# One encoder layer on one core: w_xq's transposes over four PSUM banks, w_xo's middle pieces in the weight ring, sums of x's third chunk behind a cast, and the patterns' sums turned a step later

## The chip, the cores and the metric

The kernel runs on one core of one Trainium2 chip. Time is device time in microseconds (us). The core has TensorE (PE; its weight loads are PEld), VectorE (DVE), ScalarE (ACT), GpSimd (POOL) and SyncE (SP), which work off their own queues in order, and sixteen DMA engines. SP issues most transfers and POOL the rest; a transfer that waits holds up all that is queued behind it on its issuer.

## The reference

One layer of a bidirectional encoder over 2048 tokens of width 1024, in float32:

```python
y = rmsnorm(x, g_mix) @ w_in                     # q, k, v (8 heads of 64) and the conv's a, g
att = sum over 3 dilated window patterns of weights * attention(q, k, v)
conv = silu(layernorm(depthwise_conv31(a * sigmoid(g))))
h = x + concat(att, conv) @ w_out
xq = rmsnorm(h, g_x) @ w_xq                      # 4 heads of 256
xk, xv = rmsnorm(mem, g_mem) @ w_xk, ... @ w_xv  # 256 memory tokens
h = h + softmax(xq xk^T / 16) xv @ w_xo
h = h + square(relu(rmsnorm(h, g_mlp) @ w_up)) @ w_down
out = rmsnorm(h, g_final)
```

The weights of the patterns are a softmax over the logarithms of the three patterns' denominators.

## The kernel before

Matrix products are made in three passes from a high and a low part of each operand (hi x hi, lo x hi, hi x lo: `mm3`, L270 to L272). A high part is a cast on ScalarE (`xh`, `whi`, `lwhi`), a low part a subtraction on VectorE or GpSimd (`xl`, `wlo`, `lwlo`).

The tokens go in four chunks of 512 (numbered 0 to 3; what the change's title calls the third chunk is `xprep(sp, 2)`). For a chunk, `xprep` loads x, sums its squares on ScalarE (L381, tile `junk`), makes the inverse root `rsx` on VectorE, spreads it over partitions by TensorE transposes (`rb`, copied to `rbs`), transposes x (`xt`), stores the transposed x (`xts` to `xscr`, by SP), and multiplies and splits it into `xh` and `xl`. The input linear then makes 128 columns of w_in for a chunk at a time: `glu` units (a and g columns; `sig` is the sigmoid of g's columns and `u` the product), then q and k (kr and qr are the columns that rope turns), then v. `linear` takes a PSUM bank of the kind "mm"; the bank is free again when its reader (`sig`, `u`, a rope operation) is done.

`qkscale` reads the q and k columns of w_in once more, in 16 loads by SP (tiles `qks`), squares them on ScalarE (L781) and sums the partitions on TensorE (`qkp`, L789); the scale of the q and k weights comes from that. `mem` prepares the memory tokens.

The order in each queue is written by hand. The work is given as Python generators; `weave(main, (side, rate))` takes a step of main and then rate steps of each side, `pinned(gen, names)` puts a generator's instructions behind the ones that `last` holds under these names, and `after` does it for one block. A simulated timeline then sets the order of what is not pinned, so that a pin moves neighbours as well. `steps` is the stream of linear units, `later` the chunks 2 and 3 of x and the memory, `qks` the scale's generator.

In the attention stage the far patterns run with a filler beside them: the class `Matrices` makes, for cross attention, products of the weights with the memory. Its 32 pieces are 0 to 15 (w_xk and w_xv, `proj`), 16 to 23 (w_xq) and 24 to 31 (w_xo). `turn` transposes a head's two pieces of w_xq on TensorE, four 128x128 blocks to a bank (`xqt`, L539), ScalarE casts the high half (`whi_m`, L541) and VectorE makes the low half (`wlo_m`, L542), which frees the bank. `score` makes the product with the memory's keys (`pa`). `back` multiplies w_xo's pieces with the memory's values (`pb`) and stores the result (`eb` to `bscr`, by POOL). PSUM's banks in this stage are mm 0 and 1, S 3 and 4 (scores), T 5 and 6 (`pt`, the transposed probabilities, and `catT`) and O 7 and 2.

`load` brings a piece into the ring "raw" of the pool `wp`, which has two slots, or for some pieces into tiles of their own in the pool `bl`, which is opened when the filler has ended. `split` casts the piece and makes its low half (`whi_m` L261, `wlo_m` L262). After `backs` come the first two pieces of w_out (`ahead`, `raw_o`, `whi_o`) in the same ring "raw".

`combine` sums the three patterns of a head pair `pr` and a chunk `p`: it loads two of them (`ld`), works out the weights (`ce`, `csm`) and the sum (`cat`) on GpSimd, transposes it on TensorE (`catT`, L1178) and splits it (`ct`) for the product with w_out. Chunk 0 is done in the stage above; for 1 to 3 it runs beside the later stages.

Of the kernel before, what the change touches and what calls it, by code (L numbers as in the profile page):

```python
# [24 lines left out]
H = 8  # L25
# [22 lines left out]
def hybrid_layer(ctx, tc, A, out):  # L48
# [27 lines left out]
    last = {}  # L76
# [31 lines left out]
    def drain(*gens):  # L108
        for g in gens:
            for _ in g:  # L110
                pass
# [345 lines left out]
    class Matrices:  # L457
# [8 lines left out]
        def load(self, i):  # L466
            if i >= 32 or i in self.ring:
                return
            if 25 < i < 30:
                raw = self.bl.tile([P, 2, 512], F32, tag=f"rb{i}", name=f"raw_m{i}")  # L470
            else:
                raw = wp.tile([P, 8, P] if i < 24 else [P, 2, 512], F32, tag="raw", name=f"raw_m{i}", bufs=2)
            if i < 24:
                src = wcols((w_xk, w_xv, w_xq)[i // KC], i % KC * P)
            else:
                h, nh = divmod(i - 24, 2)
                src = w_xo[256 * h:256 * h + 256, 512 * nh:512 * nh + 512].rearrange("(e p) m -> p e m", p=P)
            dma(raw, src, nc.gpsimd)
            self.ring[i] = raw
# [50 lines left out]
        def turn(self, h):  # L530
            self.wt = []
            for e in range(2):
                i = 16 + 2 * h + e
                raw = self.ring.pop(i)
                whi, wlo = (wp.tile([P, 8, P], F32R, tag=f"w{q}", name=f"w{q}_m{i}", bufs=2) for q in ("hi", "lo"))
                for g in range(2):
                    pt = ps("mm", f"xqt{i}{g}")
                    for x in range(4):
                        PE.transpose(pt[:, x * P:(x + 1) * P], raw[:, 4 * g + x, :], ident)  # L539
                    hv = whi[:, 4 * g:4 * g + 4, :].rearrange("p a b -> p (a b)")  # L540
                    ACT.copy(hv, pt)  # L541
                    DVE.tensor_tensor(wlo[:, 4 * g:4 * g + 4, :].rearrange("p a b -> p (a b)"), pt, f(hv),  # L542
                                      op=ALU.subtract)
                    yield
                self.load(i + 2)
                self.wt.append((whi, wlo))
# [18 lines left out]

        def back(self, i):
            h, nh = divmod(i - 24, 2)
            if i < 26:
                self.load(i + 6)
            wh, wl = self.ring.pop(i)  # L570
            vt = self.vt
            for mc in range(2):
                ms = slice(mc * P, (mc + 1) * P)
                pt = ps("mm", f"pb{h}{nh}{mc}")
                for e in range(2):
                    mm3(pt, vt[h][:, 0, e, ms], vt[h][:, 1, e, ms], wh[:, e], wl[:, e], e == 0, e == 1)
                if mc == 0:
                    self.split(i + 1)
                ev = zp.tile([P, 512], F32, tag=f"z{(2 * i + mc) % 8}", name=f"eb{h}{mc}{nh}")
                if mc:  # L580
                    DVE.tensor_scalar(ev, pt, rmem[:, 1:2], None, op0=ALU.mult)
                else:
                    ACT.activation(ev, pt, AF.Copy, scale=rmem[:, 0:1])
                dma(bscr[4 * nh:4 * nh + 4, :, 2 * h + mc, :].rearrange("m p c -> p m c"),
                    ev.rearrange("p (m c) -> p m c", c=P), nc.gpsimd)
                yield
# [348 lines left out]
    with ExitStack() as st:  # L935
        sp = pool("stage", stack=st)
        cwt = conv_weights()
        next(cwt)
        setup()
        four = glu_first(sp, (0, 1))  # L940
        x0, x1 = xprep(sp, 0), xprep(sp, 1)
        next(four)
        next(x0)
        next(four)
        next(x1)
        next(four)
        next(four)
        next(four)
        next(four)
        next(cwt)  # L950
        x0, x1 = pinned(x0, "pgain", "gain"), pinned(x1, "pgain", "gain")
        next(x0)
        behind("sumsq", pinned(four, "rsx0"))
        behind("split", four)
        with ExitStack() as st0:
            after(st0, "rbt0", "rsx0")
            next(four)
        next(x0)
        pins = {1: (), 3: ("x0_3",), 5: ("xt0_5", "xv0_4"), 6: ("x0_5",)}
        for k in range(KC - 1):  # L960
            behind(f"x0_{k}", x1)
            next(x0)
            if k in pins:
                with ExitStack() as st0:
                    after(st0, *pins[k])
                    next(four)
        drain(x0)
        with ExitStack() as st0:
            after(st0, "x0_6", "xt0_7")
            drain(cwt)  # L970
        next(x1)
        behind("x0_6", four)
        with ExitStack() as st0:
            after(st0, "xt0_7", "xv0_6")
            next(four)
        next(x1)
        next(four)
        last["flo"] = last["lo"]
        early01 = (0, 1)
        units = [four] + [u for c in range(2, 4) for u in glu(c, early01)]  # L980
        units += [lin_qk(isq, c) for c in ("r", 0, 1, 2) for isq in (False, True)]
        ready = {}

        def hook():
            ready["gated"] = pipeline(*(u for c in range(4) for u in glu(c, (2, 3), True)))
            next(ready["gated"])
            ready["mats"] = Matrices()

        steps = pipeline(*units, lin_v(hook), stage={0: 4})
        with ExitStack() as st0:  # L990
            after(st0, "rb1", "xl0_3")
            next(steps)
        drain(islice(steps, 10))
        weave(islice(steps, 20), (x1, 0.5))
        drain(x1)
        mem = memory(sp)
        later = pinned(chain(xprep(sp, 2), islice(mem, 1), xprep(sp, 3), mem), "x1_7", "flo", "pe")
        qks = pinned(qkscale(), "x1_7", "xs1")
        weave(islice(steps, 34), (later, 0.4), (qks, 0.2))
        weave(islice(steps, 7), (later, 2.4), (qks, 0.7))  # L1000
        drain(later, qks)
    with ExitStack() as st0:
# [118 lines left out]
    def combine(p, pr, o0):  # L1121
# [48 lines left out]
                W.tensor_tensor(at, at, src, op=ALU.add)  # L1170
        yield
        yield
        ct = [cats[0][x, pr] if end else aq.tile([P, 512], F32R, tag=f"ct{x}", name=f"ct{x}{p}{pr}") for x in "hl"]
        with ExitStack() as st:
            after(st, "pe", "act", "dve")
            pt = ps("T", f"catT{p}{pr}")
# [175 lines left out]
    with ExitStack() as st:  # L1352
        p2_ = pool("att_far", stack=st, side="right")
        qlow3 = low_parts(p2_, S, 2, "ql3")
        gated, mats = ready["gated"], ready["mats"]
# [3 lines left out]
        def filler():  # L1359
# [6 lines left out]
            for h in range(XH):  # L1366
                yield from mats.turn(h)
                yield from islice(gated, 8)
                yield from mats.score(h)
            mats.split(24)  # L1370
            yield from gated

        def backs():
# [31 lines left out]
        xp_ = pool("post_x", stack=dense)  # L1405
        with ExitStack() as st1:
            mats.bl = pool("back_w", stack=st1)
            for i in range(26, 30):
                mats.load(i)
            load_cat(0, 0)  # L1410
            load_cat(0, 1)
            weave(pinned(backs(), "pe"), (first, 0.55))
# [639 lines left out]
```

## Time and profile before

| | |
|---|---|
| three runs, median | 2781.64 us (2779.82 to 2792.18) |
| the profiled execution | 2778.42 us, its span 2776.6 us |
| mean granted TensorE clock | 0.993 |
| HBM traffic over the span | 384.46 MB read, 148.52 MB written |

The profile is of one execution. Rows of the timeline have start and length in us, engine, line, operation, tile written and tiles read, and in brackets the idle time before it with what ended it; a row with x3 stands for three in a stretch, and the length is then that of all. The tables of windows give length, busy time of each engine (with the number of instructions), granted clock, share of the sixteen DMA engines and GB/s. The input linear's stage is the first 390 us, attention with its filler 390 to 655 us, `backs` about 655 to 690 us, and w_out starts after that.

### The profile page before, as it was taken

The page shows a single profiled execution, that of the slowest core. Times are in us where ns is not written, and L with a number is a line of the kernel's source. Part 1 is how long each engine was busy: PE and PEld are TensorE (multiplying, and loading weights), DVE is VectorE, ACT ScalarE, POOL GpSimd, SP SyncE. Part 2 cuts the span into 40 slices and gives each one's busy share as a digit, 9 for nine tenths or more (in the row PEclk, how much of TensorE's full clock was granted, in tenths as well). Part 3 has the DMA queues.
Part 4 walks back from the last instruction along what each step waited for, and adds up shares of the span by engine and source line. Part 5 has one row for each costly group of instructions (what it writes and reads, how often), then busy time and mean ns, then how long its engine had stood idle before and what let it go on. Part 6 is the DMA issues. An engine that isn't in the chain of part 4 may idle for free.

```text
span 2776.6 us, 40568 instructions
## 1 busy us (share of the span) xinstructions
PE 2686.4 (97%) x14783; PEld 2073.0 (75%) x14783; DVE 1905.0 (69%) x3485; ACT 1261.7 (45%) x2162; POOL 588.0 (21%) x807
## 2 busy tenths in 40 slices
PE   7999999998999999999999999999999999999998
PEld 4444457776778888787888788887887788878787
DVE  4678726665798776588985588665566776666765
ACT  6742227655454333434544434454344444444435
POOL 6564323543002212201111101121010122200000
PEclk9999999999999999999999999999999999999999
DMA  7875457887536666766467777764434554484553
GB/s 255 229 189 117 132 183 194 255 244 235 179 115 208 214 221 202 241 212 202 133 206 228 247 224 232 238 217 152 138 114 144 186 193 163 166 300 152 164 181 106
DMA packets 459816, 535.67 MB, mean 193 GB/s; under 512 B 98173, under 2 KB 329201, under 8 KB 459617
## 3 DMA queue, kind: packets, MB, share of 16 engines
q1 hardware_dynamic: 420992, 406.52, 48.6%
q0 software_dynamic: 36752, 123.06, 12.6%
q10 hardware_dynamic: 1872, 3.52, 0.3%
q8 instruction: 116, 1.90, 0.3%
q14 instruction: 84, 0.68, 0.1%
HBM read 384.46 MB, written 148.52 MB: 192 GB/s over the span
## 4 chain that ended last, share of the span: by engine, by line
PE 69%; DMA 9%; issue 8%; DVE 7%; ACT 3%; POOL 3%; SPq 2%; ACTq 0%; POOLq 0%; DVEq 0%
PE b L1750 7%; PE dn L270 4%; PE dn L271 4%; PE dn L272 4%; PE up L270 3%; PE up L272 3%; PE up L271 3%; PE lin L270 2%; PE lin L272 2%; PE lin L271 2%; PE pt L1038 2%; SPq L57 2%; PE s L1231 2%; PE x L271 1%; PE x L270 1%
## 5 line engine op out<-in xcount | busy, mean ns | idle before, releaser
L287 DVE SCALAR_TENSOR_TENSOR cacc<-cu,cwu,cacc 128x512 f32<-128x512 f32 x480 | 396.7, 828 | 6.5
L1032 ACT ACTIVATE sm<-sm,o 128x256 f32<-128x256 f32 (+1 forms) x384 | 160.0, 467 | 112.2 <-DVE o L1031 111.9
L270 PE MATMUL up<-mh,whi_u 128*128 128x512 f32 x512 | 203.9, 398 | 0.0
L270 PE MATMUL dn<-hhh,whi_d 128*128 128x512 f32 x512 | 201.6, 404 | 1.1 <-ACT hhh L1586 1.1
L271 PE MATMUL dn<-hhl,whi_d 128*128 128x512 f32 x512 | 199.9, 393 | 0.8 <-DVE hhl L1587 0.8
L272 PE MATMUL up<-mh,wlo_u 128*128 128x512 f32 x512 | 200.0, 391 | 0.0
L271 PE MATMUL up<-ml,whi_u 128*128 128x512 f32 x512 | 199.7, 390 | 0.0
L272 PE MATMUL dn<-hhh,wlo_d 128*128 128x512 f32 x512 | 198.9, 391 | 0.0
L1031 DVE CUSTOM_DVE_ANT_0 sm<-s,mask 128x256 f32<-128x256 f32 (+1 forms) x384 | 127.0, 375 | 29.7 <-PE s L1231 11.1
L1042 DVE TENSOR_TENSOR pl<-pt,ph 128x512 f16<-128x512 f32 x160 | 109.8, 687 | 48.4 <-ACT ph L1041 48.0
L247 POOL TENSOR_TENSOR nr<-st_v,mhalf 128x4 f32<-128x4 f32 x12 | 13.5, 1126 | 596.4 <-DVE st_v L243 596.4
L1601 DVE TENSOR_TENSOR h<-h,dn 128x512 f32<-128x512 f32 x128 | 86.4, 684 | 69.8 <-PE dn L272 69.2
L1041 ACT CAST ph<-pt 128x512 f16<-128x512 f32 x160 | 92.6, 579 | 78.9 <-PE pt L1038 78.1
L272 PEld LDWEIGHTS up<-mh,wlo_u 128*128 128x128 f32 x512 | 96.1, 188 | 20.4
L272 PEld LDWEIGHTS dn<-hhh,wlo_d 128*128 128x128 f32 x512 | 96.2, 188 | 20.1
L271 PEld LDWEIGHTS dn<-hhl,whi_d 128*128 128x128 f32 x512 | 96.4, 188 | 19.5 <-DVE hhl L1587 1.7
L271 PEld LDWEIGHTS up<-ml,whi_u 128*128 128x128 f32 x512 | 96.3, 188 | 18.6
L270 PEld LDWEIGHTS up<-mh,whi_u 128*128 128x128 f32 x512 | 96.2, 188 | 18.6
L270 PEld LDWEIGHTS dn<-hhh,whi_d 128*128 128x128 f32 x512 | 95.3, 188 | 19.7 <-ACT hhh L1586 2.2
L270 PE MATMUL o<-cath,whi_o 128*128 128x512 f32 x256 | 102.6, 402 | 3.3 <-ACT whi_o L261 2.5
L271 PE MATMUL o<-catl,whi_o 128*128 128x512 f32 x256 | 101.0, 395 | 1.7 <-DVE catl L1181 1.7
L270 PE MATMUL x<-pth,whi_b 128*128 128x512 f32 x256 | 100.4, 398 | 2.4 <-ACT xp L1510 1.4
(632 smaller groups left out, 7975.2 us busy)
## 6 DMA issues: line engine op xcount, KB each, us to landing
raw_u<-in_w_up_dram SPq DMA_DIRECT2D x64, 512.0 KB
raw_d<-in_w_down_dram SPq DMA_DIRECT2D x64, 512.0 KB
k<-kscr SPq DMA_DIRECT2D x32, 640.0 KB
raw_a<-ascr SPq DMA_DIRECT2D x32, 512.0 KB
raw_b<-bscr SPq DMA_DIRECT2D x32, 512.0 KB
lou<-wlo_u POOLq DMA_DIRECT2D x32, 512.0 KB, 5.5
lod<-wlo_d POOLq DMA_DIRECT2D x32, 512.0 KB, 5.7
wlo_u<-lou SPq DMA_DIRECT2D x32, 512.0 KB
```

The source lines that it names most:

```text
L57: return (q or nc.sync).dma_start(o, i)
L270: PE.matmul(o, lh, rh, start=first, stop=False)
L271: PE.matmul(o, lh, rl, start=False, stop=False)
L272: last["pe"] = PE.matmul(o, ll, rh, start=False, stop=end)
L287: DVE.scalar_tensor_tensor(acc, u[:, t:t + 512], cwu[:, c, t:t + 1], acc, op0=ALU.mult, op1=ALU.add)
L1031: last["dve"] = DVE.tensor_tensor_reduce(dst, so, mask[:, 256 * m:256 * m + nk], 1.0, 3e38, ALU.add, ALU.min, mn)
L1032: last["act"] = ACT.activation(dst, dst, AF.Exp, bias=mn, scale=-1.0)
L1038: last["pe"] = PE.transpose(pt[:, j, :], sm[:, j, :], ident)
L1041: ACT.copy(ph, pt)
L1042: DVE.tensor_tensor(pl, pt, ph, op=ALU.subtract)
L1601: last["dve"] = DVE.tensor_tensor(hs[m], hs[m], pt, op=ALU.add)
L1750: PE.matmul(o, w[i][:, k, :], Y[b][q][k], start=first and k + x == 0, stop=k == 3 and x == 2, skip_group_check=not first)
```

## The change

Four edits, apart from each other:

```diff
@@ load
-            if 25 < i < 30:
+            if i > 27:
                 raw = self.bl.tile([P, 2, 512], F32, tag=f"rb{i}", name=f"raw_m{i}")
@@ turn
-                    pt = ps("mm", f"xqt{i}{g}")
+                    pt = ps("T" if g else "mm", f"xqt{i}{g}")
@@ back
-            if i < 26:
-                self.load(i + 6)
             wh, wl = self.ring.pop(i)
...
                     self.split(i + 1)
+                    if i == 24:
+                        self.load(27)
@@ the input linear's order
         drain(islice(steps, 10))
+        last["g2"] = last["split"]
         weave(islice(steps, 20), (x1, 0.5))
...
-        later = pinned(chain(xprep(sp, 2), islice(mem, 1), xprep(sp, 3), mem), "x1_7", "flo", "pe")
+        later = pinned(chain(xprep(sp, 2), islice(mem, 1), xprep(sp, 3), mem), "x1_7", "g2", "flo", "pe")
...
-        weave(islice(steps, 34), (later, 0.4), (qks, 0.2))
+        weave(islice(steps, 8), (later, 0.4))
+        weave(islice(steps, 26), (later, 0.4), (qks, 0.32))
@@ combine
         yield
         yield
+        if p and pr < H // 2 - 1:
+            yield
@@ filler
             mats.split(24)
+            mats.load(26)
@@ before backs
-            for i in range(26, 30):
+            for i in range(28, 32):
                 mats.load(i)
```

**The third edit on ScalarE.** In the early stage, behind the casts of x's second chunk, ScalarE has these rows before (numbers behind names are the program's; `ssx2` and `ssx3` are the sums of the chunks 2 and 3, g20 a piece of w_in's g columns):

```order
L381 ACTIVATE junk_934,ssx2_933<-xn2_0_0_911 128x512
L381 ACTIVATE junk_936,ssx2_933<-xn2_0_1_912 128x512
L381 ACTIVATE junk_938,ssx2_933<-xn2_1_0_915 128x512
...
L781 ACTIVATE qks00_960,qka_959<-qks00_960 128x512
L381 ACTIVATE junk_942,ssx2_933<-xn2_2_0_919 128x512
L781 ACTIVATE qks01_963,qka_959<-qks01_963 128x512
L381 ACTIVATE junk_944,ssx2_933<-xn2_2_1_920 128x512
L381 ACTIVATE junk_946,ssx2_933<-xn2_3_0_923 128x512
L381 ACTIVATE junk_948,ssx2_933<-xn2_3_1_924 128x512
L381 ACTIVATE junk_1276,ssx3_1275<-xn3_0_0_1211 128x512
L226 CAST lwhi_g20_693<-lraw_g20_679 128x1024
L672 ACTIVATE sig0_1_988<-lin_899,wscl_328 128x512
```

and after the change these:

```order
L226 CAST lwhi_g20_693<-lraw_g20_679 128x1024
L381 ACTIVATE junk_934,ssx2_933<-xn2_0_0_911 128x512
L672 ACTIVATE sig0_1_981<-lin_899,wscl_328 128x512
L381 ACTIVATE junk_936,ssx2_933<-xn2_0_1_912 128x512
L781 ACTIVATE qks00_1003,qka_1002<-qks00_1003 128x512
L225 ACTIVATE lraw_a20_691<-lraw_a20_691,wscl_328 128x1024
L781 ACTIVATE qks01_1006,qka_1002<-qks01_1006 128x512
L381 ACTIVATE junk_938,ssx2_933<-xn2_1_0_915 128x512
L781 ACTIVATE qks10_1030,qka_1002<-qks10_1030 128x512
L781 ACTIVATE qks11_1033,qka_1002<-qks11_1033 128x512
L226 CAST lwhi_a20_1253<-lraw_a20_691 128x1024
L781 ACTIVATE qks20_1072,qka_1002<-qks20_1072 128x512
```

The cast `lwhi_g20` and `sig0_1` come to the head, the squares of chunk 2 are spread out behind them, and qks reads and the scaling and cast of a20 come among them; the squares of chunk 3 come later. On TensorE `qkp` moves ahead by 140 rows, to the front of the g3 linear, and `rb2` back by some 250. On SP the stores of chunk 2's first two transposes (`xts2`) come ahead of the first qks load. The transposes of x's chunk 3 move back into the linears kr1 to kr3, and the last `rope_qr` of VectorE's rows near 186 us comes eleven rows earlier.

**The second edit on POOL.** Before, from the last store of `ascr` to the first piece of w_out (the sums of the patterns and two stores of u between them left out):

```order
L57 DMA ascr_110<-ea33_7195 128x2x256
L57 DMA raw_m30_7798<-in_w_xo_dram 128x2x512
L57 DMA raw_m31_7834<-in_w_xo_dram 128x2x512
...
L57 DMA bscr_111<-eb000_7811 128x4x128
L57 DMA bscr_111<-eb010_7821 128x4x128
L57 DMA raw_m26_7772<-in_w_xo_dram 128x2x512
L57 DMA raw_m27_7774<-in_w_xo_dram 128x2x512
L57 DMA raw_m28_7776<-in_w_xo_dram 128x2x512
L57 DMA raw_m29_7778<-in_w_xo_dram 128x2x512
L57 DMA bscr_111<-eb001_7847 128x4x128
...
L57 DMA bscr_111<-eb201_7998 128x4x128
L57 DMA raw_o00_8093<-in_w_out_dram 128x8x128
```

After:

```order
L57 DMA ascr_110<-ea33_7195 128x2x256
L57 DMA raw_m26_7205<-in_w_xo_dram 128x2x512
L57 DMA raw_m27_7811<-in_w_xo_dram 128x2x512
...
L57 DMA bscr_111<-eb000_7813 128x4x128
L57 DMA bscr_111<-eb010_7823 128x4x128
L57 DMA raw_m28_7774<-in_w_xo_dram 128x2x512
L57 DMA raw_m29_7776<-in_w_xo_dram 128x2x512
L57 DMA raw_m30_7778<-in_w_xo_dram 128x2x512
L57 DMA raw_m31_7780<-in_w_xo_dram 128x2x512
L57 DMA raw_o00_8093<-in_w_out_dram 128x8x128
L57 DMA bscr_111<-eb001_7847 128x4x128
L57 DMA bscr_111<-eb011_7857 128x4x128
L57 DMA raw_o01_8099<-in_w_out_dram 128x8x128
```

The two early loads are pieces 26 and 27 in place of 30 and 31, the four at the start of `backs` are 28 to 31, and the first piece of w_out comes nine rows earlier, directly behind them.

**The first edit on TensorE.** The transposes of pieces 16 and 17 in the attention stage before (matmuls only, whole groups shortened to their first row):

```order
L539 MATMUL xqt160_5825<-ident_307,raw_m16_5654 128x128 x4
L1231 MATMUL s_5832<-k3_3_4990,qh3_3_4992 128x256
...
L1038 MATMUL pt_5849<-ident_307,sm_5763 128x128 x4
L1046 MATMUL opt_5787<-v2_01_4978,ph_5783 128x65
...
L539 MATMUL xqt161_5842<-ident_307,raw_m16_5654 128x128 x4
...
L539 MATMUL xqt170_5876<-ident_307,raw_m17_5747 128x128 x4
L539 MATMUL xqt171_5883<-ident_307,raw_m17_5747 128x128 x4
L270 MATMUL lin_5919<-xh0_2_903,lwhi_g22_5206 128x512
```

and after:

```order
L539 MATMUL xqt160_5825<-ident_307,raw_m16_5654 128x128 x4
L1235 MATMUL s_5832<-k3_3_4990,qh3_3_4992 128x256
...
L539 MATMUL xqt161_5842<-ident_307,raw_m16_5654 128x128 x4
L1048 MATMUL opt_5787<-v2_01_4978,ph_5783 128x65
...
L1040 MATMUL pt_5849<-ident_307,sm_5763 128x128 x4
L1050 MATMUL opt_5787<-v2_01_4978,pl_5784 128x65
...
L539 MATMUL xqt170_5876<-ident_307,raw_m17_5747 128x128 x4
L1101 MATMUL s3_5893<-k3_4_5519,qh3_4_5521 128x128
...
L539 MATMUL xqt171_5883<-ident_307,raw_m17_5747 128x128 x4
```

`xqt161` moves ahead of `pt` and of its `opt` group, `xqt170` ahead of the scores `s3`, and `xqt171` behind six matmuls of the linear.

The fourth edit moves `catT` and its split a few units later for chunks 1 to 3 and the first three head pairs.

## The prediction

> **What bounds the kernel now.** I read the page first, then the chain's view, TensorE's waits, a table of windows, and the timelines of the stretches where the waits are.
>
> ```profile
> span 2776.6 us, 40568 instructions
> PE 2686.4 (97%) x14783; PEld 2073.0 (75%) x14783; DVE 1905.0 (69%) x3485; ACT 1261.7 (45%) x2162; POOL 588.0 (21%) x807
> PE 69%; DMA 9%; issue 8%; DVE 7%; ACT 3%; POOL 3%; SPq 2%; ACTq 0%; POOLq 0%; DVEq 0%
> ```
>
> TensorE is busy for 97% of the span and carries 69% of the chain that ended last. The change neither adds nor removes a matmul, so it can only win or lose time in which TensorE stands still or runs at half clock. The view of TensorE's waits (total, times, longest) gives the prices that the four edits can touch:
>
> ```profile
> PE xqt L539 <- DVE wlo_m L542: 6.1, 5, 1.8
> PE catT L1178 <- POOL cat L1170: 4.9, 3, 2.2
> PE pb L270 <- ACT whi_m L261: 4.1, 1, 4.1
> PE lin L270 <- ACT sig L672: 3.8, 1, 3.8
> PE rb L255 <- DVE rsx L250: 2.6, 2, 1.5
> PE o L270 <- ACT whi_o L261: 2.5, 1, 2.5
> PE lin L270 <- DVE rope_qr L874: 2.3, 1, 2.3
> PE pb L271 <- DVE wlo_m L262: 0.8, 1, 0.8
> ```
>
> Some waits cost more than their length, because the granted clock falls behind them. Four short windows (length; PE, PEld, DVE, ACT, POOL busy; clock; DMA share; GB/s) follow the sig wait, the rope_qr wait, the whi_m wait and the whi_o wait:
>
> ```profile
> 76.50:79.90 3.40, 3.21 (x10) 1.73 (x11) 2.15 (x8) 3.40 (x9) 1.06 (x2) 0.50 0.82 239
> 189.10:192.50 3.40, 3.20 (x8) 1.14 (x8) 3.33 (x4) 2.49 (x5) 3.40 (x3) 0.50 0.82 191
> 663.60:670.40 6.80, 6.07 (x16) 4.47 (x17) 2.75 (x4) 2.53 (x3) 0.75 (x1) 0.50 0.98 345
> 690.90:694.30 3.40, 3.40 (x9) 2.62 (x9) 3.04 (x5) 1.04 (x1) 0.86 (x1) 0.50 1.05 329
> ```
>
> At a clock of 0.50 half the window is lost: 1.7, 1.7, 3.4 and 1.7 us. A wait of 2.3 us lost the clock here as one of 4.1 did. The Trainium skill ("TensorE: Matmul & The Clock Gate", Part 1) says that the clock halves after at least one idle window of about 3.4 us; by that rule the 2.3 us and 2.5 us waits would have kept it, and the new wait that I find below would cost no clock. The trace speaks against it, so I keep 1.7 us as a possible surcharge on any wait over 2.3 us.
>
> **The early stage (third edit).** First TensorE, then ScalarE, then SP's queue with ScalarE's waits for qks in all (us, times), in before:
>
> ```profile
> 70.52 0.38 PE L271 MATMUL lin<-xl,fhi_a 128*128 128x512 f16 x1
> 70.73 0.38 PE L272 MATMUL lin<-xh,flo_a 128*128 128x512 f16 x1
> 70.95 0.28 PE L213 MATMUL sqs_a<-sqv_a,small 128*128 128x1 f32 x2
> 75.03 0.38 PE L270 MATMUL lin<-xh,lwhi_g 128*128 128x512 f16 x1 [3.81 <-ACT sig L672]
> 76.69 1.11 PE L255 MATMUL rb<-ident,rsx 128*128 128x128 f32 x4 [1.06 <-DVE rsx L250]
> ```
>
> ```profile
> 62.47 0.62 ACT L381 ACTIVATE junk<-xn 128x512 bf16<-128x512 f32 x1
> 68.58 0.63 ACT L781 ACTIVATE qks<-qks 128x512 f32<-128x512 f32 x1 [3.13 <-DMA qks<-in_w_in_dram]
> 73.37 1.03 ACT L226 CAST lwhi_g<-lraw_g 128x1024 f16<-128x1024 f32 x1
> 74.30 0.68 ACT L672 ACTIVATE sig<-lin,wscl 128x512 f32<-128x512 f32 x1
> 76.79 1.15 ACT L225 ACTIVATE lraw_a<-lraw_a,wscl 128x1024 f32<-128x1024 f32 x1
> 85.17 1.05 ACT L208 ACTIVATE sqj_a<-lraw_a 128x1024 bf16<-128x1024 f32 x1
> 104.06 0.19 ACT L781 ACTIVATION_READ_ACCUMULATOR qks<-qks 128x1 f32 x1
> ```
>
> ```profile
> 61.65 1.07 SPq L57 DMA_DIRECT2D qks<-in_w_in_dram  x2
>   DMA qks<-in_w_in_dram: 7.1, 3
> ```
>
> From 62.47 ScalarE works off x's squares (junk), waits 3.13 us for the first qks piece, and only then makes lwhi_g and sig. TensorE stands still for 3.81 us, then 1.06 us for x2's rsx, and loses 1.7 us of clock: 6.6 us. After the change lwhi_g and sig stand at the head of that stretch and rb comes some 250 TensorE rows later, so these 6.6 us go. What is late next?
>
> (a) The second bank. The next linear's second bank is freed by u (DVE), which now stands behind the column chain from sqs_a at 70.95. TensorE would want the bank at about 71.6; I allow 1 us, an estimate, 0 to 2.
>
> (b) qkp. It moves ahead by 140 rows, from behind the g3 linear's first half to its very front. A linear's matmul starts every 0.215 us (70.52, 70.73), and between sqs_a and qkp now stand 96 of them, 20.7 us: TensorE arrives at 71 + 1 + 20.7 = 92.7 us. The last of the product with the sig's bank lies 7 matmuls before sqs_a, so sig can run at about 69.5 us. From there until lwhi_g's next cast, ScalarE has 4 sigs at 0.6 (2.4), 6 squares at 0.8 with their accumulator reads (4.8), 16 qks at 0.65 (10.4), two scalings at 1.1 (2.2), one square of a column at 1.05, and two casts at 0.95 (1.9): 22.8 us, so 92.3 us with nothing to wait for, and 1.2 us for the cast's low half: 93.5. But the qks loads start later: on SP they now stand behind the stores of x2's first two transposes, which stand 23 matmuls and a set of transposes before sqs_a, at 65.5 us; with copy and issue, 66.5 instead of 61.65. In before the first load was read 6.9 us after its issue (61.65 to 68.58), so the first read comes at 73.4 instead of about 71, and the end goes to about 95.3. TensorE waits 2.6 us. Ends: 0, if loads come in time; 6.5, if qks waits again for DMA in between. The clock surcharge of 1.7 may come with it.
>
> (c) x's third chunk. Its transposes, sums and casts move into the kr linears, and the kr3 linear reads it. Sixteen VectorE operations, each of a size with the rope_qr row's 0.68 us (below), so 11 us, stand between the first rope and the last of them, and two linears of 24 matmuls, 10.4 us, is the time they have. I take 2 us, 0 to 5.
>
> Sum of the early stage: -6.6 + 1 + 2.6 + 2 = -1.0 us, from -6.6 to +8.6.
>
> A second effect is on the 186 us wait. VectorE stood in two taps when rope_qr came up:
>
> ```profile
> 184.35 4.29 DVE L287 SCALAR_TENSOR_TENSOR cacc<-cu,cwu,cacc 128x512 f32<-128x512 f32 x2
> 188.57 0.68 DVE L874 TENSOR_TENSOR rope_qr<-lin,rope_qr 128x512 f32<-128x512 f32 x1
> ```
>
> The last rope_qr now stands 11 rows earlier on VectorE, ahead of five taps and the v scale's column work. The 2.3 us and their 1.7 us of clock can go; I take 3 us, 0 to 4.
>
> **w_xq's transposes (first edit).** Each matrix has two groups of four transposes; the next group's bank comes free when VectorE has made the low half (wlo_m) of the one two groups back. TensorE, then VectorE:
>
> ```profile
> 553.50 0.63 PE L539 MATMUL xqt<-ident,raw_m 128*128 128x128 f32 x4 [0.38 <-PE s L1231]
> 555.43 0.63 PE L539 MATMUL xqt<-ident,raw_m 128*128 128x128 f32 x4 [1.30 <-DVE wlo_m L542]
> 554.61 1.28 DVE L542 TENSOR_TENSOR wlo_m<-xqt,whi_m 128x512 fp32r<-128x512 f32 x2
> ```
>
> With four banks the last group no longer needs the first's. 6.1 us are in the row of waits; four heads hold most of it. What it pays: pt uses the same T pair, so a pt now follows the previous pt's low half (pl). In the new order pt stands after the two matmuls that need only the high half, and the next one needs pl anyway, so the wait would come there without it. I take 5 us, 2 to 6.1.
>
> **w_xo's pieces (second edit).** POOL's issues, and the cast that waited:
>
> ```profile
> 656.71 2.83 POOL L57 DMA_DIRECT2D raw_m<-in_w_xo_dram  x4
> 680.01 0.91 POOL L57 DMA_DIRECT2D raw_o<-in_w_out_dram  x1
> 661.97 1.04 ACT L261 CAST whi_m<-raw_m 128x1024 fp32r<-128x1024 f32 x1 [2.73 <-DMA raw_m<-in_w_xo_dram]
> ```
>
> Piece 26 was issued at 656.71, landed with the cast's start at 661.97, and TensorE stood for it: 4.1 + 0.8 us and 3.4 us of clock, 8.3 us. Pieces 26 and 27 now go where 30 and 31 went, some fifteen POOL rows ahead of that issue, so this goes. The four pieces that are issued at 656.71 are then 28 to 31, wanted only after the matmuls of 26 and 27. raw_o moves ahead on POOL too, from behind nine bscr stores to just behind the four pieces: whi_o's 2.5 us and 1.7 us of clock could go as well, 12.5 us in all. Against it stands the DMA table:
>
> ```profile
> 660.00:695.00 35.00, 27.84 (x136) 21.07 (x137) 19.79 (x38) 15.04 (x21) 12.74 (x17) 0.85 1.01 359
> 695.00:720.00 25.00, 22.26 (x120) 17.36 (x118) 14.98 (x31) 10.13 (x17) 3.54 (x4) 1.00 0.80 240
> ```
>
> The sixteen engines are full for 35 us and 0.80 full for 25 more; 5 us are idle in them. If all that they carry must land before the w_out matmuls go on, no more than 5 us can be won; if the tail can wait, 12.5. I take 7, nearer to the lower end, since shares of 1.01 leave no room; 0 to 12.5. The Trainium skill ("DMA: Bandwidth & Descriptors", Queues, rings and completion order) says that each DMA engine goes round robin between the queues that have work, a packet at a time; by that rule an earlier raw_o takes its turns from SP's loads, and the term would be the 5 rather than the 12.5.
>
> **Sums of patterns (fourth edit).** The extra step moves catT only for p of 1 to 3 and the first three head pairs. The row of catT's waits holds three, 4.9 us, all of the last head pair, which the edit leaves alone: 0 us (-2 to +3, by the longest catT wait, 2.2, either way and some for a later store of cath).
>
> **The sum.** -1.0 - 3 - 5 - 7 + 0 = -16 us. Against the profiled execution's own 2778.4 us (span 2776.6) that is 2762.4; the median of the runs lies 3.2 above that execution, so in its terms 2781.6 - 16 = 2765.6, rounded to 2766.
>
> **Rivals.** First: the DMA takes the second edit back. With the engines full, the pieces of w_out or the cat halves become the wait, the second edit's term is 2 rather than 7 us, and the whole is -11: 2771. For it: shares of 1.01 over 35 us. Against: the four pieces and raw_o are 2.6 MB, and 359 GB/s over 35 us are 12.6 MB.
>
> Second: the early stage loses what it saves, and more. The waits at qkp and x3 come at their upper ends with the clock (+8.6), the 186 us wait stays: -12 + 8.6, 2778. For it: ScalarE's queue ends within 3 us of TensorE's arrival, on paper. Against: ScalarE waited for qks in only three of sixteen.
>
> Third, slower: qks paces TensorE. In before the sixteen reads took from 68.58 to 104.06, 35.5 us, and nobody minded, as qkp came later. If they still take that long from 73.4, qkp comes at 108.9, 16.2 us after TensorE arrives; cast and low half 2.1, clock 3.4, x3 5 late behind it on ScalarE. With the 1 us of (a): -6.6 + 1 + 16.2 + 2.1 + 3.4 + 5 = +21; less 5 for xqt and 2 for the pieces, +14: 2796. It decides when the last qks is read after 92.7 + 16 = 109 us. Against: those reads were spread by the order, which now puts them closer.
>
> That the fourth edit does nothing at all is in the sum already.
>
> **How the numbers follow.** About 0.5%, 13.9 us, is what a measurement of this kernel can tell from no change: faster is below 2767.7, slower above 2795.5. The forecast has 0.54 (its own range 2754 to 2772; 0.42 of it faster, 0.12 within); the first rival 0.18 (0.03 faster, 0.15 within), the second 0.12 (0.01 and 0.11), the third 0.16 (0.06 within, 0.10 slower). That gives 0.46, 0.44 and 0.10. The range goes from 2753 to 2790: it reaches through the second rival and leaves out the gains above 28 us and most of the third.
>
> **What would show it.** In the trace after: no 3.8 us wait for sig near 71 us; a wait before qkp, near 93 us, of 0 to 6.5 us; xqt's waits under 2 us in all; no wait for whi_m near 659 us and a clock of 1.00 there; between 660 and 720 us a DMA share still near 1; catT's waits as before. Wrong would be a wait before qkp above 10 us, a wait for whi_o or catl that takes the 8.3 us over, or a kr3 linear that stands for x3 longer than 5 us.

## The result and the profile after

Median of six runs 2809.43 us (2804.67 to 2814.1), against 2783.82 us (2777.76 to 2792.18) for six of before: ratio 1.0093 [1.0075, 1.0112]. The change makes the kernel slower by 25.6 us, where 16 us of gain were forecast.

The head of the page after, and its waits of TensorE over the span (us, times, longest):

```profile
span 2806.7 us, 40572 instructions
PE 2693.5 (96%) x14783; PEld 2076.0 (74%) x14783; DVE 1901.9 (68%) x3485; ACT 1262.7 (45%) x2162; POOL 584.5 (21%) x807
...
PE pb L270 <- ACT eb L583: 14.7, 2, 12.9
PE lin L270 <- DVE rope_kr L874: 11.0, 2, 6.4
PE opt L1050 <- DVE pl L1044: 9.8, 6, 5.8
PE lin L270 <- DVE stl_k L887: 4.5, 1, 4.5
PE rb L255 <- DVE rsx L250: 4.3, 2, 2.8
PE catT L1182 <- POOL cat L1172: 4.2, 3, 2.5
PE sqs_a L213 <- DVE qkv L790: 1.8, 1, 1.8
PE lin L270 <- ACT sig L672: 0.8, 1, 0.8
```

The waits for xqt, whi_m and rope_qr that the prediction priced are gone and the one for sig is down to 0.8 us. Four others took their place: pb for `eb`, the linear for `rope_kr` and for `stl_k`, opt for `pl`.

Where along the span the time went is read from the views of single tiles. They give the matmuls that use a weight tile (count, then shortest, median and longest in ns, first start and last end in us). Before:

```profile
L270 PE MATMUL lin<-xh,lwhi_q x96: 376/379/379, 196.1 to 301.2; 128*128 128x512 f16 x96
L270 PE MATMUL pa<-kt,whi_m x64: 279/281/390, 543.1 to 616.2; 128*128 128x256 f32 x64
L270 PE MATMUL pb<-whi_m,vt x32: 390/396/703, 651.8 to 685.7; 128*128 128x512 f32 x32
L270 PE MATMUL o<-cath,whi_o x256: 387/389/628, 689.1 to 2025.3; 128*128 128x512 f32 x128
L270 PE MATMUL up<-mh,whi_u x512: 387/389/497, 854.4 to 1803.7; 128*128 128x512 f32 x171
```

After:

```profile
L270 PE MATMUL lin<-xh,lwhi_q x96: 376/379/634, 214.9 to 321.0; 128*128 128x512 f16 x96
L270 PE MATMUL pa<-kt,whi_m x64: 279/282/562, 562.7 to 639.4; 128*128 128x256 f32 x64
L270 PE MATMUL pb<-whi_m,vt x32: 390/396/796, 676.2 to 719.2; 128*128 128x512 f32 x32
L270 PE MATMUL o<-cath,whi_o x256: 387/389/499, 720.9 to 2057.8; 128*128 128x512 f32 x128
L270 PE MATMUL up<-mh,whi_u x512: 387/389/501, 884.1 to 1836.3; 128*128 128x512 f32 x171
```

The delay is 19.8 us at the last q linear, 19.6 at the first pa, 24.4 at the first pb, 31.8 at the first matmul of w_out and 29.7 at the first of w_up. So 20 us are lost in the early stage (third edit), 5 in the stretch with w_xq (first edit) and 7 in the backs (second edit), of which 2 come back. The whole is 30.1 us here and 25.6 us by the medians, because before's profiled execution lies 5.4 us under its median. The 5 and 7 us are high readings too: from the first pa to the first pb before takes 108.7 us and from there to w_out 37.3 us, and the profiles of kernels below without the edit in question have 108.7 to 112.8 and 37.1 to 42.5 us (after: 113.5 and 44.7).

Windows of after (columns as in the prediction): three stretches of the early stage, then the windows at half clock.

```profile
60.00:120.00 60.00, 57.34 (x286) 28.54 (x285) 20.23 (x50) 40.01 (x86) 21.63 (x20) 1.00 0.83 216
120.00:180.00 60.00, 43.60 (x211) 22.16 (x210) 29.17 (x48) 30.16 (x56) 32.66 (x37) 0.90 0.70 203
180.00:225.00 45.00, 40.46 (x180) 18.18 (x179) 44.28 (x45) 18.20 (x28) 34.65 (x31) 0.95 0.55 136
...
160.60:167.40 6.80, 4.66 (x12) 1.63 (x12) 2.32 (x4) 2.31 (x3) 5.07 (x10) 0.50 1.04 392
174.30:181.10 6.80, 3.98 (x10) 1.46 (x10) 2.22 (x3) 5.14 (x8) 4.51 (x4) 0.50 0.69 164
215.20:218.60 3.40, 3.40 (x10) 1.22 (x8) 3.33 (x4) 0.00 (x0) 3.39 (x5) 0.51 0.84 139
587.30:594.10 6.80, 5.22 (x32) 5.22 (x33) 3.35 (x10) 3.01 (x6) 4.19 (x10) 0.50 0.94 184
696.50:710.10 13.60, 4.11 (x15) 3.10 (x16) 3.02 (x3) 2.61 (x4) 1.50 (x2) 0.50 0.95 363
```

Half of TensorE's busy time in a window at half clock is lost. In the early stage that is (4.66 + 3.98 + 3.40) / 2 = 6.0 us, against 3.2 us before (3.21 and 3.20, the windows that the prediction quotes). TensorE's waits between 60 and 230 us are 23.5 us after and 8.2 us before. What after has more of the two, 15.3 us of waits and 2.8 us of clock, is 18 of the 19.8 us.

### The profile page after: what moved, and what is told of

Same layout as the page of the kernel before. It is cut to its first block, busy times and chain, and to the rows that moved or that the text cites. A ratio compares the mean times of both kernels' runs of the same rounds, so it can differ in the third digit from the quotient of the medians.

```text
span 2806.7 us, 40572 instructions
## 1 busy us (share of the span) xinstructions
PE 2693.5 (96%) x14783; PEld 2076.0 (74%) x14783; DVE 1901.9 (68%) x3485; ACT 1262.7 (45%) x2162; POOL 584.5 (21%) x807
## 4 chain that ended last, share of the span: by engine, by line
PE 69%; issue 8%; DMA 7%; DVE 5%; ACT 3%; POOL 2%; SPq 1%; ACTq 0%; POOLq 0%; DVEq 0%
PE b L1755 7%; PE dn L270 4%; PE dn L271 4%; PE dn L272 4%; PE up L270 3%; PE up L272 3%; PE up L271 3%; PE lin L272 2%; PE lin L270 2%; PE lin L271 2%; PE pt L1040 2%; PE s L1235 2%; PE x L270 2%; PE x L271 2%; PE x L272 2%
## 5 line engine op out<-in xcount | busy, mean ns | idle before, releaser
L1044 DVE TENSOR_TENSOR pl<-pt,ph 128x512 f16<-128x512 f32 x160 | 109.5, 685 | 44.5 <-ACT ph L1043 44.1
L270 PE MATMUL xs<-whi_a,yh 128*128 128x512 f32 x256 | 102.3, 401 | 0.0
```

What stands on the lines that cost most here:

```text
L270: PE.matmul(o, lh, rh, start=first, stop=False)
L1044: DVE.tensor_tensor(pl, pt, ph, op=ALU.subtract)
```

## The experiments

Differences are against the kernel before unless another is named. Ratios are to before, run on the same chip.

### Each edit by itself

The first kernel has the `turn` part of the diff alone, the second `load`, `back`, the filler and `backs`, the third the input linear's order, the fourth `combine`.

> The first edit alone (second transposes of a w_xq piece in banks 5 and 6). Theory A, by the changed kernel's trace: the four waits of xqt for wlo_m (6.1 us) go, but the load of ld for the second head pair's sum now stands behind five loads of v on SP, VectorE stands for it (8.8 us there, 3.1 before) with TensorE behind it (5.9 us and 3.4 us of clock): about +2 us against before, from -2 to +5. Rival B, that the lost bank and not SP's order is at fault: pt waits for the pl of the pt before it in every group, many short waits, and the loss of ld is chance: -5 us, as predicted, or several us slower without a long wait for ld.

> The second edit alone (pieces 26 and 27 of w_xo in the ring, 28 to 31 and w_out's first pieces issued together). Theory A: ScalarE's own store of o stands 13 to 14 us for the completion of a cat load that comes 17 us after its issue, as w_out's two pieces are now ahead of it; TensorE stands 13 us in pb and loses 6.8 us of clock: +5 us against before, from +2 to +9. Rival B: the long wait in the changed kernel comes from the other edits (SP's queue arriving differently), and alone the second edit wins its 7 us.

> The third edit alone. Theory A: the input linear's stage is where most of the 26 us come from; the waits for rope_kr, stl_k and rsx and the half clock behind them return as they are: +20 us, from +15 to +24. Rival B: the stages do not add up, since a later start of a stage is made good by slack behind it: +10 us or less.

> The fourth edit alone. Theory A: its catT had no wait, so 0 us, within 3 us either way. Rival B: it moves stores of ct and loads of ld and weights on SP's queue at nine places, which costs about half a us at each: +4 to +6 us.

Measured: first edit 1.0003 [0.9988, 1.0019], second 1.0005 [0.9993, 1.0017], third 1.0065 [1.0049, 1.0082], fourth 1.0002 [0.9990, 1.0014]. The loss is the third edit's; the first two don't win what was forecast, and neither they nor the fourth can be told from no change. The four add up to 0.75%, and the 0.93% of the whole lies within what their intervals allow.

### The third edit in its two halves

Only the pin:

```diff
         drain(islice(steps, 10))
+        last["g2"] = last["split"]
...
-        later = pinned(chain(xprep(sp, 2), islice(mem, 1), xprep(sp, 3), mem), "x1_7", "flo", "pe")
+        later = pinned(chain(xprep(sp, 2), islice(mem, 1), xprep(sp, 3), mem), "x1_7", "g2", "flo", "pe")
```

> Only the pin of the third edit: the chunks 2 and 3 of x behind the cast of g2, the weave as before. x's chunk 3 is again transposed up to the kr3 linear here (last transpose at row 1096 of TensorE, 900 before the change, 1116 after it). Theory A, that the late chunk 3 makes the loss by SP's queue (its stores stand ahead of lraw_q's loads, and ScalarE stands for lraw_q in front of the rope copies): +12 to +20 us against before, with the 6 to 7 us wait for rope_kr near 172 us. Rival B, that the qks reads that moved ahead make the loss: within 4 us of before.

Only the weave:

```diff
-        weave(islice(steps, 34), (later, 0.4), (qks, 0.2))
+        weave(islice(steps, 8), (later, 0.4))
+        weave(islice(steps, 26), (later, 0.4), (qks, 0.32))
```

> Only the new weave of the third edit: no qks for eight steps and then 0.32 instead of 0.2 a step, without the pin. Chunk 3's last transpose stands at row 922 of TensorE, nearly where it was (900), and lwhi_g and sig stand behind the squares as before. Theory A: within 4 us of before, with the wait for sig near 71 us still there and none for rope_kr. Rival B, that the qks reads make the loss: +10 us or more.

Measured: pin 1.0047 [1.0028, 1.0066], weave 0.9990 [0.9975, 1.0005]. The pin alone makes 13 of the third edit's 18 us; the weave alone costs nothing that can be told. Then the changed kernel without the pin, all else in it:

```diff
-        last["g2"] = last["split"]
...
-        later = pinned(chain(xprep(sp, 2), islice(mem, 1), xprep(sp, 3), mem), "x1_7", "g2", "flo", "pe")
+        later = pinned(chain(xprep(sp, 2), islice(mem, 1), xprep(sp, 3), mem), "x1_7", "flo", "pe")
```

> The changed kernel without the pin on g2's cast; the other edits and the new weave stay. Theory A: the four singles add up without the 13 to 20 us of the pin: within 5 us of before (2782 to 2792). Rival E (the edits cost only together): still over 2797 us.

Measured 1.0017 [1.0005, 1.0030]: some 21 of the 25.6 us go with two lines.

### Is it chunk 3's place, whatever put it there?

The pin delays all of `later`: chunk 2, chunk 3 and the memory. In before, chunk 3 was held back, behind the last row of chunk 2, and with it the rest of the memory, which follows it in `later`:

```diff
-        later = pinned(chain(xprep(sp, 2), islice(mem, 1), xprep(sp, 3), mem), "x1_7", "flo", "pe")
+        later = pinned(chain(xprep(sp, 2), islice(mem, 1), pinned(xprep(sp, 3), "x2_7"), mem), "x1_7", "flo", "pe")
```

> The kernel before with x's chunk 3 (loads' use, squares, transposes) held behind the last cast of chunk 2, and nothing else: sig, qks, qkp and chunk 2 stay as they were, chunk 3's last transpose goes from row 900 to row 1008 of TensorE, between before and the pin alone (1096). Theory A (a late chunk 3 costs by itself): waits for rope_kr, rope_qr or stl_k of over 3 us between 150 and 215 us that before does not have, +6 to +14 us. Rival C (the pin's other rows): within 3 us of before.

Measured 1.0061 [1.0042, 1.0080], some 17 us: nearly the third edit's loss, and more than the 6 to 14 us expected. Its three longest waits of TensorE from 60 to 230 us:

```profile
PE lin L270 <- DVE rope_kr L874: 7.1, 1, 7.1
PE lin L270 <- ACT sig L672: 4.6, 1, 4.6
PE lin L270 <- DVE stl_k L887: 4.3, 1, 4.3
```

The sig wait of before is still there, since nothing moved it; `rope_kr` and `stl_k` are the ones that after has. Holding back chunk 3 and what follows it brings them, without the weave and with chunk 2 nearly where it was (its first `rb` at 79.2 us, 76.7 before, 102.5 after). The memory is late too: its first transpose (`mt`) is at 146.1 us, against 131.2 before and 153.2 after. No run separates a late chunk 3 from a late memory. The windows 120 to 180 and 180 to 225 us, first before, then with chunk 3 late, to be read beside those of after above (165 to 210 us is for the comparison below):

```profile
120.00:180.00 60.00, 60.00 (x296) 29.33 (x295) 35.55 (x44) 30.15 (x43) 35.06 (x36) 1.00 0.80 222
180.00:225.00 45.00, 42.30 (x191) 18.84 (x190) 38.52 (x50) 16.23 (x23) 24.24 (x25) 0.96 0.55 124
165.00:210.00 45.00, 42.51 (x192) 19.02 (x191) 44.43 (x47) 19.24 (x28) 33.30 (x30) 0.96 0.62 148
```

```profile
120.00:180.00 60.00, 52.76 (x254) 25.95 (x253) 27.82 (x48) 32.55 (x47) 31.11 (x36) 0.91 0.75 216
180.00:225.00 45.00, 40.67 (x184) 18.24 (x182) 44.50 (x49) 14.68 (x22) 27.71 (x27) 0.96 0.55 126
```

Before, TensorE has no gap from 120 to 180 us. With chunk 3 late it is idle for 7 us there, after for 16. VectorE (third busy column) does 6 to 8 us less in that stretch. From 180 to 225 us it is full, 44.3 to 44.5 of 45 us against 38.5. But the windows stand at fixed times, and by then both kernels are 13 to 20 us behind: before has 44.43 of 45 us as well, from 165 to 210 us. So a full VectorE is no mark of the loss; what is lost is its work, and TensorE's, in the stretch before.

How chunk 3 reaches the ropes is seen on ScalarE. After (start, length, idle before and what ended it):

```profile
174.01 1.15 ACT L225 ACTIVATE lraw_q<-lraw_q,qkc 128x1024 f32<-128x1024 f32 x1 [8.17 <-DMA lraw_q<-in_w_in_dram]
175.17 0.58 ACT L872 COPY sw_kr<-lin 64x512 f32<-64x512 f32 x1
```

Before:

```profile
164.58 0.58 ACT L872 COPY sw_qr<-lin 64x512 f32<-64x512 f32 x1 [1.20 <-DVE stl_kr L887]
167.21 1.15 ACT L225 ACTIVATE lraw_q<-lraw_q,qkc 128x1024 f32<-128x1024 f32 x1 [0.26 <-DMA lraw_q<-in_w_in_dram]
```

Rope reads a linear's bank through the copies `sw_kr` and `sw_qr`, and the bank is free only after them. Before, the copies for kr and the first for qr are done when the scaling of `lraw_q` comes up, and its load has just landed. After, the ropes of kr are later than that scaling in ScalarE's queue, the loads are issued later as well (161.00 to 170.49 us on SP, 158.93 to 164.57 before), and ScalarE stands for the load of this piece for 8.17 us with two ropes' kr copies behind it. TensorE waits 6.4 us for the bank. In the kernel that only holds chunk 3 back, that wait of ScalarE is 8.24 us, and the load has landed at 166.20 us, no later than before: there the copies wait by the order on ScalarE, not by a later load.

### Three changes to that path

The third edit with chunk 3's stores on POOL, so that nothing on SP stands behind them:

```diff
-            last[f"xs{n}"] = dma(xscr[k][:, 512 * n:512 * (n + 1)], xt)
+            last[f"xs{n}"] = dma(xscr[k][:, 512 * n:512 * (n + 1)], xt, nc.gpsimd if n == 3 else None)
```

> The third edit alone, with the eight stores of chunk 3's transposes (xscr) issued by POOL instead of SP. Theory A: TensorE's rows are the same as in the third edit alone, but lraw_q's loads come earlier on SP; the wait of ScalarE for lraw_q (8.2 us) and TensorE's 6.4 us for rope_kr with its 3.4 us of clock go: 8 to 10 us faster than the third edit alone, so +8 to +12 us against before. Rival C, that the late chunk itself, not the store's place, sets the rope: no change from the third edit alone, +18 us.

Measured 1.0075 [1.0047, 1.0104], no better: ScalarE still stands 7.5 us for `lraw_q`. SP's stores are not it.

The third edit with `later` at twice the rate in the second weave, so that chunk 3 comes earlier again:

```diff
-        weave(islice(steps, 26), (later, 0.4), (qks, 0.32))
+        weave(islice(steps, 26), (later, 0.8), (qks, 0.32))
```

> The third edit alone, with 0.8 instead of 0.4 steps of x's chunks to a step of the linear in the second weave. Chunk 3 comes earlier (last transpose at row 1042 of TensorE instead of 1116, before the change 900), the sig stays at the head. Theory A: the loss grows with that row, so about half of it is left: +8 to +12 us. Rival C, the loss is from qkp and the column scales that stand earlier: +18 us, as with the third edit alone.

Measured 1.0060 [1.0039, 1.0080]. In its profile the last q linear ends 8.5 us later than before (309.7 against 301.2), not some 20, yet the total is hardly better than the third edit's, where half the loss was expected to go; the later stretches lost more in it, and why is open. (One profile is a rough measure here: the kernels that leave the early stage alone end that linear between 301.2 and 304.5 us.)

The third edit with the scaling of that one `lraw_q` behind the last rope copy:

```diff
-            scaled_split(raw, sc, hi, lo, POOL)
+            with ExitStack() as st:
+                if isq and c == 1:
+                    after(st, "sw")
+                scaled_split(raw, sc, hi, lo, POOL)
...
-                ACT.copy(sw[64:128], pt[0:64])
+                last["sw"] = ACT.copy(sw[64:128], pt[0:64])
```

> The third edit alone, with ScalarE's scaling of the first lraw_q piece after qr held behind the last copy for rope (sw), so that the copies that free the linear's banks no longer stand behind a wait for a load. Theory A (the order on ScalarE carries the late chunk into TensorE's waits): TensorE's second wait for rope_kr near 172 us, 7.3 us in the third edit alone, and its clock loss of 3.4 us go; 6 to 10 us faster than the third edit alone, +9 to +13 us against before. Rival C (the copies are late through the late chunk itself): the wait stays over 4 us, and the time at +18 us.

Measured 1.0068 [1.0043, 1.0092], where 6 to 10 us less than with the third edit alone were expected. Its waits of TensorE from 60 to 230 us, then a row of SP and one of VectorE:

```profile
PE lin L270 <- DVE stl_k L890: 6.8, 1, 6.8
PE lin L270 <- DVE rope_kr L877: 6.2, 2, 4.7
```

```profile
172.71 2.31 SPq L57 DMA_DIRECT2D rope_kr<-in_rope_dram  x2
177.76 0.69 DVE L877 TENSOR_TENSOR rope_kr<-lin,rope_kr 128x512 f32<-128x512 f32 x1 [7.46 <-DMA rope_kr<-in_rope_dram]
```

With the third edit alone the two rope_kr waits are 7.2 and 4.7 us and the one for `stl_k` 5.1. Here one of the rope_kr waits goes (7.2 to 1.5), `stl_k` grows, one of 2.6 for rope_qr comes, and the total stays. The 8-us wait on ScalarE is where the time is seen in after, but not all that holds the ropes: here the last rope of kr waits 7.46 us on VectorE for its table, which SP issues only behind the four loads of `lraw_q` (162.37 to 172.27 us). Before, SP issued the last tables of kr (149.34 to 155.72 us) ahead of these loads (from 158.93); in after, too, they stand behind them, at 170.94. So the rows suggest that the late chunk holds the same rope twice, by ScalarE's order and by SP's. VectorE is not short of time there, 6.75 of 20 us busy from 160 to 180. No kernel removes both waits, so how much of the 18 us goes this way is open.

### The second edit: who waits for the transfers

ScalarE's own store of attention sums stands ahead of the cast for the next product. Before, then after:

```profile
674.70 0.38 ACT L1249 COPY o<-opt 128x260 f32<-128x260 f32 x1
675.11 0.34 ACTq L57 DMA_DIRECT2D oscr<-o  x1
```

```profile
690.34 0.38 ACT L1253 COPY o<-opt 128x260 f32<-128x260 f32 x1
703.92 0.34 ACTq L57 DMA_DIRECT2D oscr<-o  x1
704.31 1.04 ACT L261 CAST whi_m<-raw_m 128x1024 fp32r<-128x1024 f32 x1 [13.59 <-DMA catl<-catl]
```

After, the input `o` is ready at 690.72, yet the store is issued at 703.92, and what ended the wait is, by the profile, a load of `catl` that SP had issued. The two share no data, and no view shows what ties them. Before, the store went out as soon as its input was ready, 18 us after the four pieces of w_xo were issued (656.71). After, its input is ready 10 us after them (681.06), with `raw_o`'s two loads right behind them, and ScalarE's whole queue waits with the store. If that wait were the price, taking the store off ScalarE would win it back:

```diff
-                    os_.rearrange("p b h e -> p b (h e)"), None if far and pr < 3 else nc.scalar)
+                    os_.rearrange("p b h e -> p b (h e)"), None if far else nc.scalar)
```

> The second edit alone, with the last far store of o in chunk 0 issued by SP instead of ScalarE. Theory A (ScalarE's own store stands for the completion of a cat load): the 12.9 us wait of TensorE in pb goes with its 6.8 us of clock; what is left is the wait of whi_o or catl for loads. 8 to 14 us faster than the second edit alone and than before. Rival D (the full DMA engines are the bound, whoever stands for them): the wait moves to whi_m, whi_o or catl, the time stays within 4 us of before.

Measured 1.0010 [0.9997, 1.0023], no better than the edit alone. The `pb` wait falls from 12.8 to 1.7 us, and as much turns up elsewhere; TensorE's longest wait there, and a row of VectorE's timeline:

```profile
PE o L270 <- DVE eb L581: 10.3, 1, 10.3
```

```profile
704.95 0.17 DVE L1142 TENSOR_TENSOR csm<-ld 128x8 f32<-128x8 f32 x1 [14.06 <-DMA ld<-oscr]
```

Now VectorE stands for 14.06 us, for patterns that could be loaded only after that store. The 60 us from the issue of the four pieces, before, with the edit alone, and with the store on SP:

```profile
657.00:717.00 60.00, 49.02 (x261) 37.47 (x260) 34.81 (x69) 23.87 (x37) 18.40 (x24) 0.91 0.94 313
```

```profile
659.00:719.00 60.00, 42.85 (x245) 33.57 (x244) 32.07 (x68) 22.22 (x36) 19.31 (x25) 0.89 0.90 302
```

```profile
668.00:728.00 60.00, 43.22 (x232) 33.07 (x231) 31.70 (x66) 21.93 (x35) 18.78 (x25) 0.83 0.88 297
```

All move 17.8 to 18.8 MB (GB/s times 60 us) at a share of 0.88 to 0.94. Where the store stands decides which engine waits: TensorE does 6 us less than before in that stretch either way. By the ratios (+0.05% and +0.10%) 1 to 3 us of that are left at the end. That the filled DMA engines are the reason fits these shares; no run with fewer bytes in the stretch tests it.

### The first edit: one load behind five

With the first edit alone, VectorE has this wait between 500 and 620 us (second: before):

```profile
DVE csm L1142 <- DMA ld<-oscr: 10.3, 1, 10.3
```

```profile
DVE csm L1142 <- DMA ld<-oscr: 3.1, 1, 3.1
```

The reordering has put the load of one head pair's patterns (`ld`) behind five loads of v on SP; VectorE stands for it with `pl` behind, and opt waits. The cure, with the edit:

```diff
-                oscr[pr][i][512 * p:512 * (p + 1)].rearrange("(j p) e -> p j e", p=P))
+                oscr[pr][i][512 * p:512 * (p + 1)].rearrange("(j p) e -> p j e", p=P), nc.gpsimd if (p, pr) == (0, 1) else None)
```

> The first edit alone, with the two loads of ld for the second head pair issued by POOL instead of SP. Theory A (SP's order, five loads of v ahead of ld): VectorE's wait for ld falls from 9 us to under 3, TensorE's 7.4 us wait in opt and its 3.4 us of clock go; the first edit then shows its 5 to 6 us, with the total 5 to 9 us under before. Rival B: as the first edit alone, within 3 us of before.

Measured 0.9983 [0.9968, 0.9998]: the wait falls to 0.2 us and the kernel gains 0.17%, the only ratio of this study with all of its interval below 1, and by little. That is 4.7 us (0.6 to 8.9), about the 5 forecast for this edit. One interval among fifteen that just leaves out 1 can be chance, and neither of the two kernels below that contain this cure repeats the gain. A wait of 7.7 us for `whi_o` stands near 689 us in its profile, 2.5 before.

The two cures together, with the first and second edits and neither of the others:

> The first two edits with both of these moves, without the third and fourth: by theory A the sum of the two, 13 to 20 us under before (2765 to 2772); by the rivals B and D within 5 us of before.

Measured 1.0011 [0.9997, 1.0026]; a wait of 13.4 us at the first w_out product remains, in yet another place. And the first edit with its cure and the new weave, without pin, second and fourth edits:

> The first edit with ld's loads on POOL, and the third edit's weave without its pin. If the two add up as they measured alone (-0.17% and -0.10%), 4 to 9 us under before; if the full DMA engines behind 660 us take back what comes before them, within 3 us of before.

Measured 0.9991 [0.9978, 1.0004], not distinguished from before. None of these kernels beats before by more than 0.2%.

## Why the prediction was wrong

**Early stage, (a), right.** The 3.8 and 1.1 us near 71 to 77 went, and their clock: from 60 to 120 us it is 1.00. 1 us was allowed for the second bank, which u frees; the 0.8 us that came are booked to sig (waits of after, above).

**(b), right in size, not in its wait.** TensorE was to arrive at 92.7 us and wait 2.6 us at qkp, for ScalarE's reads of qks and the cast behind them:

```profile
93.47 0.28 PE L789 MATMUL qkp<-qkv,small 128*128 128x2 f32 x2
```

TensorE arrived at 93.5 us and did not wait there: the last qks was read by 92.3 us and the cast was done at 93.3. The 1.8 us came four matmuls later, before `sqs_a`, for `qkv`, a step of VectorE that (b) does not list (its row is in the last section). That the sizes agree is luck. The third rival, qks as TensorE's pace, did not happen; that it forecast a slower kernel is no support for it.

**(c), the step that failed.** It gave chunk 3, which it calls x's third chunk, 2 us in the kr linears, 0 to 5. It counted sixteen VectorE operations against the time of two linears, and asked only whether kr3 would wait for x3. It did not ask what comes late behind chunk 3 in the other queues: the memory's transposes and casts, the copies on ScalarE that free the ropes' banks and stand behind the scaling of `lraw_q`, the ropes' tables on SP. Measured behind qkp: waits of 11.0 for rope_kr, 4.5 for `stl_k`, 2.8 for rb, 1.3 each for xt and mt, and 6.0 us of clock. Holding back chunk 3 and the memory alone costs 0.61%, 17 us; which queue sets the price stays open. The third edit with its 186-us term was forecast at -4 us and is +18 (0.65%): 22 of the 41.6 us between forecast and result. The second edit is 8 and the first 6 us of it, and the rest is within the intervals.

**186 us, half right.** The wait for rope_qr went, the 4.5 us for `stl_k` came 25 us later.

**Second edit, mis-sized.** 7 us of gain forecast, 0 to 12.5; measured +0.05% [-0.07, +0.17], no gain that can be told from none. The waits that were to go, went. The first rival named the mechanism (the engines are full, the pieces or the cat halves become the wait) but gave it 2 us and 18%; the experiment with the store moved agrees with it. The Trainium skill's round robin between queues ("DMA: Bandwidth & Descriptors", Queues, rings and completion order) was read as lowering the term to 5 us; the direction agrees, the size doesn't, and no run separates the round robin from the plain fullness.

**First edit, mis-sized by its side effect.** 5 us forecast, +0.03% measured, 0.17% [0.02, 0.32] of gain with `ld` on POOL. The step checked what `pt` waits for in the new order, and not which loads SP issues in it.

**Fourth edit, right.** 0 forecast, +0.02% [-0.10, +0.14]; catT still has three waits (4.2 us, 4.9 before).

The range went to 2790, past the second rival's 2778, whose early stage took (c)'s 5 us as an end, and the third rival's 2796 took the same 5 us: the range failed by the same step.

## What to carry to other kernels

When an edit delays a chain, list for each in-order queue what stands behind the moved instructions, not just who reads their result: here the price of a late chunk 3 showed at the ropes of kr, whose copies and tables had come to stand behind other loads. Where the queues are written by hand, a pin on one generator reorders the loads on SP and the casts on ScalarE as well; compare those orders before pricing a gained wait. Where the DMA engines were 0.88 to 0.94 busy, removing a wait moved it to another engine; in such a stretch, price a removed wait at no more than the idle time that is left there until a run shows more.

## What the runs showed of the hardware

A store issued by ScalarE held that engine's arithmetic for 13.4 us (second edit alone) to 13.6 us (after), with its own input ready, until a load that SP had issued was complete. No data ties the two, and what does is open.

The length of a wait did not settle the clock. In after, the 1.8 us before `sqs_a` at 96.41 us and the 2.8 us before rb at 127.92 us were followed by a clock of 1.00; before, the 2.3 us near 189 us halved it for 3.4 us. The Trainium skill ("TensorE: Matmul & The Clock Gate", Part 1) ties the drop to an idle window of about 3.4 us. The half-clock windows here are 3.4 us or multiples of it (6.8, 13.6), which agrees; the 2.3-us case lost the clock after a shorter wait than that. The two waits in after, in TensorE's timeline (no window at half clock stands between 60 and 160 us):

```profile
96.41 0.38 PE L213 MATMUL sqs_a<-sqv_a,small 128*128 128x1 f32 x2 [1.78 <-DVE qkv L790]
127.92 0.65 PE L255 MATMUL rb<-ident,rsx 128*128 128x128 f32 x4 [2.80 <-DVE rsx L250]
```
